# Sums of an output weight's blocks: from GpSimd in SBUF to copies and accumulating transfers from DRAM to DRAM

## The chip, the cores and the metric

One core of a Trainium2 chip. The metric is the device time of one execution in microseconds (us), taken as the median of several runs. Loads, stores and the transfers between DRAM tensors (DMA) run on 16 DMA engines that all queues of the core share. The engines are called here by the names of the profile: PE (TensorE), PEld (its weight loads), DVE (VectorE), ACT (ScalarE), POOL (GpSimd) and SP (SyncE, which issues nearly all DMAs; "SPq" in the rows).

## The reference, cut to what matters

A layer with two groups of heads over 1024 tokens and a model width of 2048, all in float32:

```python
h = einsum('bsd,de->bse', x, w_in)            # 1024 x 2048 by 2048 x 5392
q_a, k_a, v_a, z_a, q_g, k_g, v_g, z_g, gk_lr = split(h, ...)
y_a = sliding_window_attention(rope(q_a), rope(k_a), v_a, sinks) * silu(z_a)
y_g = rmsnorm(gated_linear_attention(q_g, k_g, v_g, decay(gk_lr))) * silu(z_g)
y = einsum('bse,ed->bsd', concatenate([y_a, y_g], -1), w_out)   # 1024 x 2048 by 2048 x 2048
out = layer_norm(2 ** 0.25 * x + y, ln_g, ln_b)
```

## The kernel before

**Products.** Each float32 operand of a large product is split into two parts (`split`, lines 109 to 114): ACT casts it to a high part (L112), DVE subtracts that from the operand to get the low part (L113). Each product is then three matmuls, high by high, high by low and low by high.

**Input projection.** The work is a list of jobs, one column block of `w_in` each, in the order of the string `ORDER`: K V q0 k0 v0 a0 z0 and so on, once for each half of the tokens. Jobs 0 and 1 (K and V) run together; job 2 is q0, job 3 is k0, job 4 is v0. An ordinary job is 48 matmuls of 128x512 (`main_f`, L172 to L174); a job of kind "v" is 192 matmuls of 128x256 (`main_v`, L186 to L188). The weights of a job come by SP in loads of 512 KB (`load`, L103) into the four buffers `raw`, and the split parts go to the eight buffers of `w_p`, which hold two ordinary jobs' worth. Attention and the linear attention run between the jobs' matmuls on all engines.

**Output projection.** It is one level of Strassen's scheme (Winograd's form): seven products instead of eight, over the quarters of y and of `w_out`, in the order `seq = (1, 6, 7, 4, 5, 3, 2)`. Products 4 to 7 take a combination of the weight's blocks b11, b12, b21, b22; products 1 to 3 take a block as it is. y is kept in DRAM (`yd`) and loaded again; `y_part` makes the combinations of y's blocks on POOL (L721, L717), and `collect` adds the finished sums to the residual.

**The weight's combinations** are made beforehand by `weight_sums` (L626 to L639), which is called 32 times between the jobs of the projection, after every second job from job 6 on. A call loads four pieces of 128x256 (L634, 128 KB each) into one `raw` buffer, does four subtractions on POOL (L635 to L638) and stores the four results with one DMA of 512 KB to the DRAM tensor `td` (L639). In `w_part` products 4 to 7 read them from there (L736) in runs of 1 KB.

**What sets the order.** The program is handed to a scheduler, which places each instruction in its engine's queue by the program's order, by priorities (`tc.high_priority`) and by what it takes to be ready. On the chip each queue runs in order. Semaphores order what depends on each other; SP's DMAs use eight semaphores in turn, and a DMA waits until the DMA that had its semaphore before, eight DMAs ahead, has landed.

```python
def weight_sums(n):
    f, k, u = n // 16, n % 16 // 2, n % 2
    ...
    for t, (eg, q) in ((b11, (f, 0)), (b12, (2 + f, 0)), (b21, (f, 2)), (b22, (2 + f, 2))):
        SP.dma_start(t, w_out[eg, q + k // 4][:, c])
    G.tensor_tensor(b11, b12, b11, ALU.subtract)
    ...
    SP.dma_start(td[f][:, n % 16], r)
```

Of the kernel before, what the change touches and what calls it, by code (L numbers as in the profile page):

```python
# [7 lines left out]
F32 = mybir.dt.float32  # L8
# [3 lines left out]
ALU = mybir.AluOpType  # L12
# [4 lines left out]
P = 128  # L17
S = 1024
D = 2048
T = 512  # L20
# [55 lines left out]
def build(ctx: ExitStack, tc, xT, xr, w_e, w_v, w_gk, w_up, b_gk, cos_d, sin_d, cst_d, sinks, wn_d, w_out, g_d, b_d, out):  # L76
    nc = tc.nc
    V, A, G, PE, SP = nc.vector, nc.scalar, nc.gpsimd, nc.tensor, nc.sync

    raw_p = ctx.enter_context(tc.tile_pool(name="raw", bufs=4))  # L80
    w_p = ctx.enter_context(tc.tile_pool(name="wsp", bufs=8))
    x_p = ctx.enter_context(tc.tile_pool(name="xsp", bufs=16))
    dr_p = ctx.enter_context(tc.tile_pool(name="ydram", bufs=1, space=DRAM))
# [73 lines left out]
    G.tensor_copy(al, acc_a.rearrange('p c i -> p (c i)').unsqueeze(1).to_broadcast([P, NB, P]))  # L157


    td = [dr_p.tile([P, 16, 4, 256], F32, name=f"td{f}") for f in range(2)]  # L160
    ys_d = dr_p.tile([P, 8 * T], F32, name="ysum")
    yd = [[dr_p.tile([P, 4 * T], F32, name=f"yd{H}_{q}") for q in range(4)] for H in range(2)]


    def main_f(ws, xs):
        accs = [mm.tile([P, T], F32, name="acc", tag="mm") for _ in ws]
        for k in range(KT):
            xh, xl = xs[k]
            c = slice((k % 4) * P, (k % 4) * P + P)
            for acc, w in zip(accs, ws):  # L170
                wh, wl = w[k // 4]
                PE.matmul(acc, wh[:, c], xh, start=(k == 0), stop=False)  # L172
                PE.matmul(acc, wh[:, c], xl, start=False, stop=False)  # L173
                PE.matmul(acc, wl[:, c], xh, start=False, stop=(k == KT - 1))  # L174
        return accs

    def main_v(w, xs):
        acc = [mm.tile([P, 2, 256], F32, name="accv", tag="mm") for _ in range(2)]
        for k in range(KT):
            wh, wl = w[k // 2]  # L180
            c = slice((k % 2) * 256, (k % 2) * 256 + 256)
            xh, xl = xs[k]
            for tb in range(NB):
                o = acc[tb // 2][:, tb % 2]
                t = slice(tb * P, tb * P + P)
                PE.matmul(o, xh[:, t], wh[:, c], start=(k == 0 and tb % 2 == 0), stop=False, skip_group_check=True)  # L186
                PE.matmul(o, xh[:, t], wl[:, c], start=False, stop=False, skip_group_check=True)  # L187
                PE.matmul(o, xl[:, t], wh[:, c], start=False, stop=(k == KT - 1), skip_group_check=True)  # L188
        return acc
# [117 lines left out]
    def low_rank(acc, wgk, k, r):  # L307

        u = k % 4
        PE.matmul(acc[32 * u:32 * u + 32], wgk[:, 32 * k:32 * k + 32], r, start=(k < 4), stop=(k >= 12), tile_position=(0, 32 * u), skip_group_check=True)  # L310
# [132 lines left out]
    def order(ins, head):  # L443
        with_dep = mybir.DependencyInfo(mybir.DependencyClass.NoSync, mybir.DependencyReason.DATA)
        tc.add_manual_dep(ins.ins, head.ins.name, with_dep, reason="after the bank's first")
        return ins
# [120 lines left out]
    def evac_lr(H):  # L567
        acc = ctxs[H].pop("lracc")
        lr = cp.tile([P, T], F32R, name="lr", tag="lr")
        A.copy(lr, acc)  # L570
        V.scalar_tensor_tensor(lr, lr.bitcast(F32), cst[:, C_DUP:C_DUP + 1], acc, ALU.mult, ALU.add)
        ctxs[H]["lr"] = lr
# [4 lines left out]
    n = len(jobs)  # L577
# [46 lines left out]
        load_tabs(H)  # L624
        return xr

    def weight_sums(n):

        f, k, u = n // 16, n % 16 // 2, n % 2
        c = slice((k % 4) * 512 + u * 256, (k % 4) * 512 + u * 256 + 256)  # L630
        r = raw_p.tile([P, 4, 256], F32, name="raw", tag="raw")
        b11, b12, b21, b22 = r[:, 0], r[:, 1], r[:, 2], r[:, 3]
        for t, (eg, q) in ((b11, (f, 0)), (b12, (2 + f, 0)), (b21, (f, 2)), (b22, (2 + f, 2))):
            SP.dma_start(t, w_out[eg, q + k // 4][:, c])  # L634
        G.tensor_tensor(b11, b12, b11, ALU.subtract)  # L635
        G.tensor_tensor(b12, b22, b12, ALU.subtract)
        G.tensor_tensor(b22, b22, b11, ALU.subtract)
        G.tensor_tensor(b21, b21, b22, ALU.subtract)  # L638
        SP.dma_start(td[f][:, n % 16], r)  # L639

    def get(i):
        if i not in parts:
            parts[i] = [w for src in jobs[i].src for w in load_split(src, w_p, "w")]
        return parts.pop(i)
# [6 lines left out]
        for f in due:  # L651
            f()

    i = 0
    while i < n:
        H = jobs[i].H
        if i in (0, n0):
            xr0 = begin(H, i)
        group = [i, i + 1] if i in paired else [i]
        ws = [get(j) for j in group]  # L660
        if jobs[i].kind == "v":
            accs = [main_v(ws[0], ctxs[H]["x"])]
        else:
            accs = main_f(ws, ctxs[H]["x"])
        if i == 0:
            for k in range(KT):
                low_rank(ctxs[0]["lracc"], ctxs[0]["wgk"], k, xr0[k])
        if i in (0, n0):
            evac_lr(H)
        if i == 0:  # L670
            x0.close()
            gp = side.enter_context(tc.tile_pool(name="gp", bufs=1, reuse_waits="tile"))
        run_later()
        for j, acc in zip(group, accs):
            if jobs[j].evac:
                jobs[j].evac(acc)
            for at, f in enumerate(jobs[j].later):
                if f and at == 0:
                    f()
                elif f:  # L680
                    pending.append((at - 1, f))
        if i > 5 and i % 2 == 0 and i // 2 - 3 < 32:
            weight_sums(i // 2 - 3)
        i += len(group)
    while pending:
        run_later()
# [14 lines left out]
    def y_raw(h, g, k, tag):  # L701

        r = x_p.tile([P, T], F32, name="yr", tag=tag)
        with tc.high_priority(2000):
            SP.dma_start(r, yd[h][2 * g + k // 4][:, (k % 4) * T:(k % 4 + 1) * T])
        return r

    def y_part(i, k):

        at = {1: "00", 2: "01", 3: "01", 4: "11", 5: "10", 6: "10", 7: "00"}[i]  # L710
        a = y_raw(int(at[0]), int(at[1]), k, "xh")
        kept = ys_d[:, k * T:k * T + T]
        if i == 3:
            b = x_p.tile([P, T], F32, name="yr", tag="xl")
            with tc.high_priority(2000):
                SP.dma_start(b, kept)
            G.tensor_tensor(a, a, b, ALU.subtract)  # L717
        more = {5: ((1, 1, 1),), 6: ((1, 1, 1), (0, 0, -1)), 7: ((1, 0, -1),)}
        for n, (h, g, sign) in enumerate(more.get(i, ())):
            b = y_raw(h, g, k, "xl" if n % 2 == 0 else "xh")  # L720
            G.tensor_tensor(a, a, b, ALU.add if sign > 0 else ALU.subtract)  # L721
        if i == 6:
            A.dma_start(kept, a)
        return split(a, x_p, "x")

    def w_part(i, fp, q, pool, tag):

        r = raw_p.tile([P, 2, 512], F32, name="raw", tag="raw")
        with tc.high_priority(2000):
            if i in (1, 2, 3):  # L730
                eg, w = {1: (fp, 0), 2: (fp, 2), 3: (2 + fp, 2)}[i]
                src = w_out[eg, w + q // 2][:, (q % 2) * 1024:(q % 2) * 1024 + 1024]
                SP.dma_start(r, src.rearrange("p (u c) -> p u c", u=2))
            else:
                j = {5: 0, 7: 1, 4: 2, 6: 3}[i]
                SP.dma_start(r.rearrange("p u (h c) -> p (u h) c", h=2), td[fp][:, 4 * q:4 * q + 4, j])  # L736
        return [split(r[:, u], pool, tag) for u in range(2)]

    def product(acc, y, w, t, k, first, last):
# [44 lines left out]
    def collect(i, fp, t, acc):  # L784
        lo, hi = slice(fp * 512, fp * 512 + 512), slice(1024 + fp * 512, 1024 + fp * 512 + 512)
        c11, c12, c21, c22 = pre[t][:, lo], pre[t][:, hi], pre[NB + t][:, lo], pre[NB + t][:, hi]
        if i == 1:
            V.scalar_tensor_tensor(c11, c11, ALPHA, acc, ALU.mult, ALU.add)
        elif i == 6:
            A.copy(c12, acc)  # L790
        elif i == 7:
            A.copy(c22, acc)
        elif i == 4:
            V.scalar_tensor_tensor(c21, c21, ALPHA, acc, ALU.mult, ALU.add)
            stat(NB + t, fp)
        elif i == 5:
            V.tensor_tensor(c22, c22, acc, ALU.add)
            stat(NB + t, 2 + fp)
        elif i == 3:
            V.tensor_tensor(c12, c12, acc, ALU.add)  # L800
            stat(t, 2 + fp)
        else:
            V.tensor_tensor(c11, c11, acc, ALU.add)
            stat(t, fp)
# [15 lines left out]
    for n, i in enumerate(seq[:-1]):  # L820
        if i in (1, 4):
            for t in range(NB):
                tb = t + (NB if i == 4 else 0)
# [30 lines left out]
    for ts in ((0, 1), (2,), (3,)):  # L854
        acc = {(t, fp): a for t in ts for fp, a in zip(range(2), banks(2))}
# [56 lines left out]
```

## Time and profile before

| | |
|---|---|
| time, median of 3 runs | 1437.69 us (1437.56 to 1438.25) |
| the profiled execution: time | 1435.88 us |
| its span, first to last instruction | 1433.7 us |
| PE busy | 1414.9 us, 99% |
| DVE, ACT, POOL busy | 856.7, 600.3, 290.3 us |
| moved by DMA | 222.36 MB |

The profile is of one execution, whose own time is 2.2 us more than its span and 1.8 us less than the median of the runs. In its rows a time is that of the instruction's start, from the span's start; "x2" after an instruction says that so many stand together. A matmul's shown duration reaches beyond the start of the next one, since matmuls are pipelined: the pace is read from the distance of the starts. A line number belongs to kernel.py before the change.

### The profile page before, as it was taken

How to read it: one execution, taken by the hardware profiler on the slowest of the kernel's cores; microseconds unless marked ns; L12 is line 12 of the kernel's file. 1: busy time of each engine (PE TensorE's matmuls, PEld its weight loads, DVE VectorE, ACT ScalarE, POOL GpSimd, SP SyncE). 2: the span in 40 equal slices, each digit the busy share in tenths (PEclk: the TensorE clock that was granted, in tenths of full speed). 3: DMA queues.
4: the chain of work that ended last, by engine and by line, in shares of the span. 5: the costliest groups of instructions: out<-in, count | busy, mean ns of one | idle time of the engine just before them, and what ended most of it. 6: DMA issues, size and time to landing. Idle time of an engine off the chain costs nothing.

```text
span 1433.7 us, 23435 instructions
## 1 busy us (share of the span) xinstructions
PE 1414.9 (99%) x8992; PEld 1181.0 (82%) x8992; DVE 856.7 (60%) x1481; ACT 600.3 (42%) x1279; POOL 290.3 (20%) x325
## 2 busy tenths in 40 slices
PE   8999999999999999999999999999999999999996
PEld 5888889888888976898888888988898888888885
DVE  5565556555655566565655555564566645466798
ACT  5544435435443445344435443443545324433320
POOL 0032212221311122213212221131101412122000
PEclk9999999999999999999999999999999999999998
DMA  8243344443434435543443334433325797665552
GB/s 318 86 148 128 111 147 131 135 133 107 144 131 134 133 127 175 168 157 113 159 133 123 115 131 136 138 112 118 104 95 163 239 362 230 216 218 189 172 208 117
DMA packets 99231, 222.36 MB, mean 155 GB/s; under 512 B 10800, under 2 KB 43568, under 8 KB 97968
## 3 DMA queue, kind: packets, MB, share of 16 engines
q1 hardware_dynamic: 97968, 218.78, 46.1%
q10 hardware_dynamic: 1152, 2.10, 0.4%
q8 instruction: 70, 1.15, 0.3%
q14 instruction: 41, 0.34, 0.1%
HBM read 180.47 MB, written 35.65 MB: 151 GB/s over the span
## 4 chain that ended last, share of the span: by engine, by line
PE 98%; DVE 1%; DMA 1%; ACT 0%; POOL 0%; SPq 0%; issue 0%; DVEq 0%; POOLq 0%
PE acc L172 18%; PE acc L174 18%; PE acc L173 17%; PE acco L742 7%; PE acco L743 7%; PE acco L744 7%; PE accv L186 4%; PE accv L188 4%; PE accv L187 4%; PE po L291 2%; PE pa L360 1%; PE ps L259 1%; PE ps L260 1%; PE pt L281 1%; PE lracc L310 1%; PE pg L405 1%
## 5 line engine op out<-in xcount | busy, mean ns | idle before, releaser
L113 DVE TENSOR_TENSOR wl<-raw,wh 128x512 fp32r<-128x512 f32 x440 | 331.6, 759 | 280.7 <-ACT wh L112 258.1
L112 ACT CAST wh<-raw 128x512 fp32r<-128x512 f32 x440 | 269.8, 620 | 416.9 <-PE acc L173 283.5
L172 PE MATMUL acc<-xh,wh 128*128 128x512 f32 x1088 | 429.4, 396 | 6.5 <-ACT wh L112 6.5
L174 PE MATMUL acc<-xh,wl 128*128 128x512 f32 x1088 | 427.1, 393 | 0.0
L173 PE MATMUL acc<-xl,wh 128*128 128x512 f32 x1088 | 426.9, 393 | 0.0
L172 PEld LDWEIGHTS acc<-xh,wh 128*128 128x128 f32 x1088 | 205.0, 188 | 53.8 <-ACT wh L112 8.4
L174 PEld LDWEIGHTS acc<-xh,wl 128*128 128x128 f32 x1088 | 204.8, 188 | 44.8 <-issue 1.4
L173 PEld LDWEIGHTS acc<-xl,wh 128*128 128x128 f32 x1088 | 205.0, 188 | 42.6 <-issue 2.2
L743 PE MATMUL acco<-wl,xh 128*128 128x512 f32 x416 | 161.9, 389 | 0.0
L742 PE MATMUL acco<-wh,xh 128*128 128x512 f32 x416 | 160.7, 390 | 0.2
L744 PE MATMUL acco<-wh,xl 128*128 128x512 f32 x416 | 160.8, 389 | 0.0
L186 PE MATMUL accv<-wh,xh 128*128 128x256 f32 x512 | 145.3, 284 | 0.0
L188 PE MATMUL accv<-wh,xl 128*128 128x256 f32 x512 | 145.0, 283 | 0.0
L187 PE MATMUL accv<-wl,xh 128*128 128x256 f32 x512 | 144.8, 283 | 0.0
L186 PEld LDWEIGHTS accv<-wh,xh 128*128 128x128 f32 x512 | 98.1, 192 | 1.2 <-issue 0.7
L188 PEld LDWEIGHTS accv<-wh,xl 128*128 128x128 f32 x512 | 98.1, 192 | 0.6 <-issue 0.3
L187 PEld LDWEIGHTS accv<-wl,xh 128*128 128x128 f32 x512 | 98.2, 192 | 0.5
L742 PEld LDWEIGHTS acco<-wh,xh 128*128 128x128 f32 x416 | 78.1, 188 | 17.3 <-ACT xh L112 1.3
L744 PEld LDWEIGHTS acco<-wh,xl 128*128 128x128 f32 x416 | 78.1, 188 | 16.7 <-DVE xl L113 0.4
L743 PEld LDWEIGHTS acco<-wl,xh 128*128 128x128 f32 x416 | 78.1, 188 | 15.8
L113 DVE TENSOR_TENSOR xl<-yr,xh 128x512 fp32r<-128x512 f32 x56 | 38.5, 687 | 77.4 <-ACT xh L112 76.9
L112 ACT CAST xh<-yr 128x512 fp32r<-128x512 f32 x56 | 34.6, 620 | 118.4 <-POOL yr L721 66.9
(169 smaller groups left out, 1686.7 us busy)
## 6 DMA issues: line engine op xcount, KB each, us to landing
raw<-in_w_e_dram SPq DMA_DIRECT2D x134, 512.0 KB, 3.9
yr<-yd SPq DMA_DIRECT2D x88, 256.0 KB, 4.8
raw<-in_w_v_dram SPq DMA_DIRECT2D x32, 512.0 KB, 4.2
raw<-in_w_out_dram SPq DMA_DIRECT2D x128, 128.0 KB, 2.7
td<-raw SPq DMA_DIRECT2D x32, 512.0 KB, 3.5
raw<-td SPq DMA_DIRECT2D x32, 512.0 KB, 4.6
raw<-in_w_out_dram SPq DMA_DIRECT2D x24, 512.0 KB, 4.0
raw<-in_xT_dram SPq DMA_DIRECT2D x15, 512.0 KB, 4.7
```

Source lines behind the costliest of these rows:

```text
L112: A.copy(hi, src)
L113: V.tensor_tensor(lo, src, hi.bitcast(F32), ALU.subtract)
L172: PE.matmul(acc, wh[:, c], xh, start=(k == 0), stop=False)
L173: PE.matmul(acc, wh[:, c], xl, start=False, stop=False)
L174: PE.matmul(acc, wl[:, c], xh, start=False, stop=(k == KT - 1))
L186: PE.matmul(o, xh[:, t], wh[:, c], start=(k == 0 and tb % 2 == 0), stop=False, skip_group_check=True)
L187: PE.matmul(o, xh[:, t], wl[:, c], start=False, stop=False, skip_group_check=True)
L188: PE.matmul(o, xl[:, t], wh[:, c], start=False, stop=(k == KT - 1), skip_group_check=True)
L291: x = PE.matmul(po[64 * u:64 * u + 64, a:b], vt[:, j + 1, 64 * g:64 * g + 64], pms[u][:, a2:b2], start=(len(heads) < 2), stop=(j == NB - 1 ...
L742: PE.matmul(acc, yh[:, c], wh, start=(first and k == 0), stop=False, skip_group_check=True)
L743: PE.matmul(acc, yh[:, c], wl, start=False, stop=False, skip_group_check=True)
L744: PE.matmul(acc, yl[:, c], wh, start=False, stop=(last and k == 7), skip_group_check=True)
```

## The change

The sums are made without SBUF and without POOL's arithmetic. Each of the 16 tensors `td[i, f, q]` (128x2048 float32, 1 MB, for product i in 5, 7, 6, 4, half f of the columns and half q of the rows) is begun by one plain copy of 1 MB of `w_out` from DRAM to DRAM, issued by SP (`sum_begin`, in the program after every third job from job 6 on), and ended by one accumulating transfer of 1 MB from DRAM to DRAM, issued by POOL (`sum_end`, after every third job from job 11 on). Transfers only add, so where a difference was needed, the signs move to the sums of y (`y_part`, add and subtract change places, as many operations as before) and to the copies from PSUM (`collect`, `A.mul` by -1 for `A.copy`). `w_part` reads the sums in runs of 4 KB. The call `order(...)` behind the accumulating transfer is a hint to the scheduler without a semaphore: it places the transfer behind the head of a job's matmuls.

```diff
-    td = [dr_p.tile([P, 16, 4, 256], F32, name=f"td{f}") for f in range(2)]
+    td = {(i, f, q): dr_p.tile([P, 4 * T], F32, name=f"td{i}{f}{q}") for i in (4, 5, 6, 7) for f in range(2) for q in range(2)}
...
-    def weight_sums(n):
-
-        f, k, u = n // 16, n % 16 // 2, n % 2
-        c = slice((k % 4) * 512 + u * 256, (k % 4) * 512 + u * 256 + 256)
-        r = raw_p.tile([P, 4, 256], F32, name="raw", tag="raw")
-        b11, b12, b21, b22 = r[:, 0], r[:, 1], r[:, 2], r[:, 3]
-        for t, (eg, q) in ((b11, (f, 0)), (b12, (2 + f, 0)), (b21, (f, 2)), (b22, (2 + f, 2))):
-            SP.dma_start(t, w_out[eg, q + k // 4][:, c])
-        G.tensor_tensor(b11, b12, b11, ALU.subtract)
-        G.tensor_tensor(b12, b22, b12, ALU.subtract)
-        G.tensor_tensor(b22, b22, b11, ALU.subtract)
-        G.tensor_tensor(b21, b21, b22, ALU.subtract)
-        SP.dma_start(td[f][:, n % 16], r)
+    sums = [(i, f, q) for i in (5, 7, 6, 4) for f in range(2) for q in range(2)]
+
+    def sum_begin(i, f, q):
+        eg, c = {5: (f, q), 7: (2 + f, q), 6: (2 + f, 2 + q), 4: (f, 2 + q)}[i]
+        SP.dma_start(td[i, f, q], w_out[eg, c])
+
+    def sum_end(i, f, q, behind):
+        src = {5: w_out[2 + f, q], 7: w_out[2 + f, 2 + q], 6: td[5, f, q], 4: td[6, f, q]}[i]
+        order(G.dma_start(td[i, f, q], src, accum_op=ALU.add, max_dma_last_dim=4096), behind)
...
-        if i > 5 and i % 2 == 0 and i // 2 - 3 < 32:
-            weight_sums(i // 2 - 3)
+        if i > 5 and i % 3 == 0 and started < len(sums):
+            sum_begin(*sums[started])
+            started += 1
+        if i > 8 and i % 3 == 2 and ended < started:
+            sum_end(*sums[ended], job_head[0])
+            ended += 1
...
+        first, *more = {1: ((0, 0),), 2: ((0, 1),), 3: ((0, 1),), 4: ((1, 1),), 5: ((1, 0), (1, 1)),
+                        6: ((1, 0), (1, 1), (0, 0)), 7: ((0, 0), (1, 0))}[i]
+        a = y_raw(*first, k, "xh")
         if i == 3:
...
+            G.tensor_tensor(a, a, b, ALU.add)
+        for n, (h, g) in enumerate(more):
+            b = y_raw(h, g, k, "xl" if n % 2 == 0 else "xh")
             G.tensor_tensor(a, a, b, ALU.subtract)
...
-                j = {5: 0, 7: 1, 4: 2, 6: 3}[i]
-                SP.dma_start(r.rearrange("p u (h c) -> p (u h) c", h=2), td[fp][:, 4 * q:4 * q + 4, j])
+                src = td[i, fp, q // 2]
+            SP.dma_start(r, src[:, (q % 2) * 1024:(q % 2) * 1024 + 1024].rearrange("p (u c) -> p u c", u=2))
...
         elif i == 6:
-            A.copy(c12, acc)
+            A.mul(c12, acc, -1.0)
         elif i == 7:
-            A.copy(c22, acc)
+            A.mul(c22, acc, -1.0)
```

The order of the instructions moves at two places. The first is SP's queue right behind the loads of the first jobs' weights and of the tables cos and sin. Before, the load of job 3's weights (`raw<-in_w_e_dram`) and of job 4's (`raw<-in_w_v_dram`) stand there:

```order
L560 DMA sin<-in_sin_dram 128x512
L103 DMA raw<-in_w_e_dram 128x1024 x2
L103 DMA raw<-in_w_v_dram 128x1024 x3
L206 DMA rs<-rq 32x512 x2
L103 DMA raw<-in_w_v_dram 128x1024
L206 DMA rs<-rq 32x512 x2
```

In the changed program the scheduler has brought all 16 copies forward to this place, since they wait for nothing that the program makes. Behind sin come first seven more rows like the first one here (`td_114` to `td_117` and `td_122` to `td_124`):

```order
L636 DMA td_125<-in_w_out_dram 16x16384
L103 DMA raw<-in_w_e_dram 128x1024
L636 DMA td_118<-in_w_out_dram 16x16384
L103 DMA raw<-in_w_e_dram 128x1024
L636 DMA td_119<-in_w_out_dram 16x16384
L636 DMA td_120<-in_w_out_dram 16x16384
L636 DMA td_121<-in_w_out_dram 16x16384
L636 DMA td_110<-in_w_out_dram 16x16384
L636 DMA td_111<-in_w_out_dram 16x16384
L636 DMA td_112<-in_w_out_dram 16x16384
L636 DMA td_113<-in_w_out_dram 16x16384
L103 DMA raw<-in_w_v_dram 128x1024 x2
```

So the first half of job 3's weights stands behind 8 copies, the second half behind 9, and job 4's behind all 16.

The second place is POOL's queue at the first sums. `s<-s,sm` is the scaling of the attention's probabilities, which PE transposes next. Before, the four subtractions of a call stand around it:

```order
L635 TENSOR_TENSOR raw<-raw 128x256
L278 TENSOR_TENSOR s<-s,sm 128x512
L636 TENSOR_TENSOR raw<-raw 128x256
L637 TENSOR_TENSOR raw<-raw 128x256
L638 TENSOR_TENSOR raw<-raw 128x256
L208 TENSOR_TENSOR rs<-rs,sin 128x512
```

In the changed program single accumulating transfers stand there, 16 in the whole queue:

```order
L282 TENSOR_TENSOR s<-s,sm 128x512
L640 DMA td_114<-in_w_out_dram 256x1024
L282 TENSOR_TENSOR s<-s,sm 128x512
L212 TENSOR_TENSOR rs<-rs,sin 128x512
L640 DMA td_115<-in_w_out_dram 256x1024
L282 TENSOR_TENSOR s<-s,sm 128x512 x2
```

Each takes the place of two calls' eight subtractions.

## Rows read from the trace of the kernel before

**Rows 1.** The page: span, then busy time of each engine, share and instructions.
```profile
span 1433.7 us, 23435 instructions
PE 1414.9 (99%) x8992; PEld 1181.0 (82%) x8992; DVE 856.7 (60%) x1481; ACT 600.3 (42%) x1279; POOL 290.3 (20%) x325
```
**Rows 2.** The waits of PE: line, releaser: us in total, times, longest.
```profile
PE acc L172 <- ACT wh L112: 6.5, 1, 6.5
```
**Rows 3.** The chain of waits at both ends: start us, us, what.
```profile
1.18 4.62 DMA raw<-in_w_e_dram
5.82 0.63 ACT wh L112
6.49 0.80 PE acc L172
...
1416.15 0.69 DVE pre L803
```
**Rows 4.** The timeline of SP, first loads and last stores: start, length, what.
```profile
19.94 0.33 SPq L139 DMA_DIRECT2D wn<-in_wn_dram  x1
...
22.51 0.33 SPq L560 DMA_DIRECT2D sin<-in_sin_dram  x1
23.83 1.25 SPq L103 DMA_DIRECT2D raw<-in_w_e_dram  x2
...
1381.37 5.76 SPq L768 DMA_DIRECT2D out_dram<-pre  x4
```
**Rows 5.** DMA issues: count, KB each, median us from issue to landing.
```profile
rs<-rq SPq DMA_DIRECT2D x72, 64.0 KB, 3.6
...
sin<-in_sin_dram SPq DMA_DIRECT2D x1, 256.0 KB, 4.4
...
wn<-in_wn_dram SPq DMA_DIRECT2D x1, 1.0 KB, 6.1
```
**Rows 6.** Windows: stretch, length, busy time of each engine, clock, DMA share, GB/s.
```profile
15.00:20.00 5.00, 5.00 (x25) 2.76 (x24) 3.98 (x7) 4.22 (x9) 0.00 (x0) 1.00 1.00 401
1390.00:1395.00 5.00, 5.00 (x24) 4.14 (x23) 5.00 (x9) 0.02 (x1) 0.00 (x0) 1.00 1.01 423
...
800.00:1000.00 200.00, 200.00 (x1321) 168.40 (x1322) 113.77 (x216) 86.31 (x198) 44.57 (x56) 1.00 0.39 129
1200.00:1360.00 160.00, 159.83 (x703) 131.25 (x702) 97.86 (x145) 59.64 (x108) 30.67 (x22) 1.00 0.65 207
```
**Rows 7.** The timeline of PE: its first matmuls, job 3's head, job 4's head.
```profile
11.35 0.63 PE L174 MATMUL acc<-xh,wl 128*128 128x512 f32 x1
11.77 0.73 PE L172 MATMUL acc<-xh,wh 128*128 128x512 f32 x2
...
48.79 0.39 PE L172 MATMUL acc<-xh,wh 128*128 128x512 f32 x1
49.02 0.39 PE L173 MATMUL acc<-xl,wh 128*128 128x512 f32 x1
...
60.64 0.29 PE L186 MATMUL accv<-wh,xh 128*128 128x256 f32 x1
```
**Rows 8.** The groups of POOL and ACT: line, what, count | busy us, mean ns.
```profile
L638 POOL TENSOR_TENSOR raw<-raw 128x256 f32<-128x256 f32 x32 | 29.7, 929 | 2.4
...
L635 POOL TENSOR_TENSOR raw<-raw 128x256 f32<-128x256 f32 x32 | 24.5, 765 | 241.6 <-DMA raw<-in_w_out_dram 227.9 <-DVE wl L113 4.6 <-DVE sza L303 4.6
...
L508 ACT ACTIVATE kq<-acc 128x512 f32<-128x512 f32 x8 | 4.7, 591 | 0.0
L790 ACT COPY pre<-acco 128x512 f32<-128x512 f32 x8 | 4.5, 588 | 1.8 <-PE acco L744 1.6
```
**Rows 9.** The timeline of POOL and of PE at one sum: the scaling, then its transposes.
```profile
123.09 1.04 POOL L278 TENSOR_TENSOR s<-s,sm 128x512 f32<-128x512 f32 x1
...
126.69 0.60 PE L281 MATMUL pt<-cst,s 128*128 128x128 f32 x4
```
**Rows 10.** The waits of SP: line, releaser: us in total, times, longest.
```profile
SPq L103 <- DVE wl L113: 287.0, 83, 9.2
```

More of the change, by code (lines that the diff above doesn't have):

```diff
@@ L157, in build @@
     G.tensor_copy(al, acc_a.rearrange('p c i -> p (c i)').unsqueeze(1).to_broadcast([P, NB, P]))
-    td = [dr_p.tile([P, 16, 4, 256], F32, name=f"td{f}") for f in range(2)]
+    td = {(i, f, q): dr_p.tile([P, 4 * T], F32, name=f"td{i}{f}{q}") for i in (4, 5, 6, 7) for f in range(2) for q in range(2)}
     ys_d = dr_p.tile([P, 8 * T], F32, name="ysum")
     yd = [[dr_p.tile([P, 4 * T], F32, name=f"yd{H}_{q}") for q in range(4)] for H in range(2)]
+    job_head = [None]
     def main_f(ws, xs):
@@ L171, in main_f @@
                 wh, wl = w[k // 4]
-                PE.matmul(acc, wh[:, c], xh, start=(k == 0), stop=False)
+                first = PE.matmul(acc, wh[:, c], xh, start=(k == 0), stop=False)
+                job_head[0] = first if k == 0 else job_head[0]
                 PE.matmul(acc, wh[:, c], xl, start=False, stop=False)
@@ L185, in main_v @@
                 t = slice(tb * P, tb * P + P)
-                PE.matmul(o, xh[:, t], wh[:, c], start=(k == 0 and tb % 2 == 0), stop=False, skip_group_check=True)
+                first = PE.matmul(o, xh[:, t], wh[:, c], start=(k == 0 and tb % 2 == 0), stop=False, skip_group_check=True)
+                job_head[0] = first if k == 0 else job_head[0]
                 PE.matmul(o, xh[:, t], wl[:, c], start=False, stop=False, skip_group_check=True)
@@ L652, in run_later @@
             f()
-    i = 0
+    i, started, ended = 0, 0, 0
     while i < n:
@@ L708, in y_part @@
     def y_part(i, k):
-        at = {1: "00", 2: "01", 3: "01", 4: "11", 5: "10", 6: "10", 7: "00"}[i]
-        a = y_raw(int(at[0]), int(at[1]), k, "xh")
         kept = ys_d[:, k * T:k * T + T]
+        first, *more = {1: ((0, 0),), 2: ((0, 1),), 3: ((0, 1),), 4: ((1, 1),), 5: ((1, 0), (1, 1)),
+                        6: ((1, 0), (1, 1), (0, 0)), 7: ((0, 0), (1, 0))}[i]
+        a = y_raw(*first, k, "xh")
         if i == 3:
@@ L716, in y_part @@
                 SP.dma_start(b, kept)
+            G.tensor_tensor(a, a, b, ALU.add)
+        for n, (h, g) in enumerate(more):
+            b = y_raw(h, g, k, "xl" if n % 2 == 0 else "xh")
             G.tensor_tensor(a, a, b, ALU.subtract)
[L718 to L721, printed above, removed]
         if i == 6:
@@ L731, in w_part @@
                 eg, w = {1: (fp, 0), 2: (fp, 2), 3: (2 + fp, 2)}[i]
-                src = w_out[eg, w + q // 2][:, (q % 2) * 1024:(q % 2) * 1024 + 1024]
-                SP.dma_start(r, src.rearrange("p (u c) -> p u c", u=2))
-            else:
-                j = {5: 0, 7: 1, 4: 2, 6: 3}[i]
-                SP.dma_start(r.rearrange("p u (h c) -> p (u h) c", h=2), td[fp][:, 4 * q:4 * q + 4, j])
+                src = w_out[eg, w + q // 2]
+            else:
+                src = td[i, fp, q // 2]
+            SP.dma_start(r, src[:, (q % 2) * 1024:(q % 2) * 1024 + 1024].rearrange("p (u c) -> p u c", u=2))
         return [split(r[:, u], pool, tag) for u in range(2)]
```

## The prediction

> **What bounds the kernel now.** I read the page first. PE is busy 1414.9 of 1433.7 us, 99%, and POOL, which the change relieves most, 20% [rows 1]. In the list of waits PE then has one wait of more than a moment: 6.5 us at the start, for the first cast of a weight [rows 2]. The chain of waits shows that this is the way of the first load: it lands at 5.8, ACT casts, PE starts at 6.49; at the other end DVE takes over from PE at 1416.15 and finishes the last row of the output [rows 3]. So the idle time of PE, 18.8 us, lies before the first matmul and behind the last one, and the change touches neither. In the output projection, where the changed loads of `td` are used, PE is busy 159.83 of 160 us [rows 6]. What can be gained there is 0.2 us; what PE loses anywhere is lost for good. The question is only whether PE has to wait for something now.
>
> The place to look at is where the new copies stand: behind sin, ahead of the weights of jobs 3 and 4. Before, sin is issued at 22.51 and lands 4.4 us later, at 26.9, and job 3's loads follow at 23.83 [rows 4, 5]. PE begins job 3 at 48.79 and job 4 at 60.64 [rows 7], so those weights had 20 us and more to spare.
>
> That a load behind the copies really waits for them is seen on the constants: `wn`, 1 KB, takes 6.1 us to land, while a rope transfer of 64 KB takes 3.6 as a rule [rows 5]. The small one was queued behind loads of 512 KB at a time when the DMA engines were fully busy, and did not overtake them. SP also issues those constants 1.3 us apart where an issue takes 0.33 [rows 4]: each waits for the landing of the DMA eight before it.
>
> **The 16 copies.** Each moves 1.049 MB. The trace has no transfer from DRAM to DRAM, so I bound it by its two legs. Loads from DRAM with all DMA engines busy move 401 GB/s (15 to 20 us); the stores of the result to DRAM, four of 1 MB, move 423 GB/s (1390 to 1395 us) [rows 4, 6]. A leg is 1.049 MB / 401 = 2.6 us for the read and 1.049 / 423 = 2.5 us for the write. If the legs overlap wholly, a copy costs 2.6 us; if DRAM does no more in both directions together than it is seen to do in one, 5.1 us. I take 5.1: a copy has both legs in DRAM, which no load and no store has, and no window shows DRAM moving more than 423 GB/s in total.
>
> A load of 512 KB at 401 GB/s takes 1.3 us, and from a landing to the first matmul it is 6.49 - 5.80 = 0.7 us [rows 3]. Then, counted from sin's landing at 26.9:
>
> - Job 3 has its first weights behind 8 copies and one load: 26.9 + 8 x 5.1 + 1.3 + 0.7 = 69.7 instead of 48.8. PE stands still for 21 us. The second half lands behind 9 copies and two loads, at 75.4 us, and is usable at 76.1; with 24 matmuls at 0.23 us behind it, job 3 ends at about 82.
> - Job 4 has its weights behind all 16 copies and three loads: 26.9 + 16 x 5.1 + 3 x 1.3 + 0.7 = 113.1 instead of 60.6. PE waits again, 31 us.
>
> The two waits do not add to more than the second arrival: the whole delay at job 4 is 113.1 - 60.6 = **52.5 us**. From there the loads come without copies between them, and as nothing on PE has slack, the delay stays until the end.
>
> The Trainium skill has a rate for such copies: "DMA: Bandwidth & Descriptors", section "Latency and other measured facts", gives 207 to 214 GB/s per direction for copies between two tensors in HBM with plain queues. An estimate by the upper figure: 4.9 us a copy, a delay of 49 us, 1489 us in all; no run here shows it yet. The same page, section "Bandwidth", puts one core's limit at the HBM at about 358 GB/s; an estimate by it, both legs one after the other and the loads at that rate too: 5.9 us a copy, a delay of 65 us, 1505 us. This case's trace does not agree with that limit: it has 401 and 423 GB/s in single windows, so the sum stays with those.
>
> **Restart.** At the start of the kernel the first 12 matmuls of PE begin 0.44 us apart ((11.77 - 6.49) / 12) and the following ones 0.23 us apart [rows 3, 7]: after its idle time PE ran at half pace for 5.3 us, although the granted clock of those windows reads 1.00. After 31 us of idle time I expect the same once more, 5.3 - 12 x 0.23 = **2.5 us**. The same restart of job 3 costs nothing, since job 4 waits for its weights anyway.
>
> **The 16 accumulating transfers on POOL.** A POOL DMA is not in the trace. For issuing one I take between the 0.33 us of an SP issue [rows 4] and the 3.4 us of the four subtractions of one call (from 0.77 to 0.93 us each [rows 8]). Each transfer replaces two calls, 6.8 us of POOL, so POOL's queue holds less in both cases: 0 on the path. What waits behind it on POOL is the scaling of the probabilities, and behind that PE's transposes; at one such place the scaling ends at 124.13 and the transposes begin at 126.69, 2.6 us later [rows 9]. That is the cover, and a POOL issue of more than 2.6 us just ahead of a scaling would be seen on PE (a rival below). The data: two reads and one write, 3 legs, some 7.6 us of the DMA engines each, 122 us in all over about 900 us of a projection in which the engines are busy 39% [rows 6]; what goes away is 32 calls of 1 MB of loads and stores, 32 x 2.6 = 83 us. Loads are mostly early: SP spent 287 us waiting until DVE freed a buffer for the next weights [rows 10]. With two jobs' worth of split weights held, a transfer of 7.6 us hides behind 11 us of matmuls per job. I cost them at 0.
>
> **Edits with one answer.** The sums of y have as many POOL operations as before, add for subtract: 0. `A.mul` for `A.copy`, 16 times: 591 against 588 ns in like shape [rows 8], off the path: 0. Loads of `td` in runs of 4 KB: at best the 0.2 us above.
>
> **Sum.** 1435.9 us (the profiled execution's own time) + 52.5 + 2.5 = 1490.9; the median of the runs is 1.8 us above that execution, so 1492.7, and I say **1492 us**.
>
> **Rivals.**
>
> 1. *The copies' legs overlap.* For it: each DMA engine reads and writes at once in any load. Against it: DRAM would have to move some 800 GB/s. At 2.6 us a copy job 3 is late by 1 us only, job 4 starts at 26.9 + 41.6 + 3.9 + 0.7 = 73.1, 12.5 us late; with the restart 15 us, **1453 us**.
> 2. *Not slower: the copies are out of the way in time.* A copy does not go through SBUF, so it might be faster than either leg as seen. The point that decides is (60.6 - 26.9 - 3.9 - 0.7) / 16 = 1.8 us a copy; below it job 4's weights are there when PE wants them, and the time stays at **1438 us**. Against it: 1.8 us is 580 GB/s in each direction, above every window of the trace.
> 3. *POOL's issue is long.* If POOL is held 3.4 us by each transfer, the scaling behind it is 0.8 us later than PE's slack allows, 16 times: 13 us more, **1505 us**. For it: in the changed order a scaling follows nearly every transfer. Against it: subtractions just as long stood there 32 times without a wait of PE.
>
> **How the numbers follow.** The forecast gets 0.67, rival 1 0.15, rival 2 0.06, rival 3 0.12. The forecast's own range takes 20% on the price of a copy for what the trace cannot show (reads beside writes, runs of 64 KB): 4.1 to 6.1 us give a delay of 36.5 to 68.5 us, 1477 to 1509. The whole range reaches down to rival 1, 1452, and up past rival 3 taken alone, to 1512; rival 2 and the far ends are left out. A difference of 0.2%, 2.9 us, is about what a measurement of this kernel tells from none. Slower by more than that: all but rival 2, 0.94. Within it 0.05, faster 0.01, since no idle time of PE is within the change's reach.
>
> **What would show it.** Right: in the waits of PE two new long ones at the heads of jobs 3 and 4, released by an ACT cast that waited for its load, some 21 and 31 us; in the windows from 27 to 110 us DMA engines fully busy and PE mostly idle; the landings of the copies 5 us apart; after job 4's head every job as late as the one before it, and a tail as long as now. Wrong: landings 2.6 us apart or less; job 4's load landing before copies issued ahead of it; waits of PE at the transposes spread over the whole projection, released by POOL (rival 3); or PE waiting for weights long after 120 us, which would mean that the accumulating transfers are not hidden.

## The result and the profile after

The changed kernel takes **1462.0 us** (4 runs, 1460.67 to 1463.0) against 1437.62 us of the kernel before beside it: a ratio of 1.0172, 95% interval 1.0155 to 1.019. It is slower, as forecast, but by 24 us and not by 54; the time lies inside the range of 1452 to 1512, a sixth of the way up, and the forecast's own range (1477 to 1509) missed it.

The page of the changed kernel, with the lines that answer to [rows 1] and the queue of POOL's DMAs (packets, MB, share of the DMA engines' time):

```profile
span 1460.8 us, 23047 instructions
...
PE 1418.9 (97%) x8992; PEld 1184.9 (81%) x8992; DVE 841.2 (58%) x1481; ACT 598.8 (41%) x1279; POOL 196.6 (13%) x213
...
q0 software_dynamic: 4352, 16.78, 6.4%
```

The span grew by 27.1 us; that is a little more than the 24 us between the medians, since the profiled execution of the kernel before was 1.8 us faster than its median. PE's busy time accounts for 4.0 of it (1418.9 for 1414.9), the rest is idle time of PE. Where, is told by the waits of PE, to be held against the single line of [rows 2]:

```profile
PE accv L189 <- ACT wh L112: 15.6, 1, 15.6
PE acc L174 <- ACT wh L112: 13.3, 2, 6.7
PE acco L746 <- ACT xh L112: 0.8, 1, 0.8
```

The two waits on L174 are the one at the start (6.6) and a new one of 6.7 us; with 15.6 and 0.8 the new ones make 23.1 us, and 23.1 + 4.0 is the 27.1. The timeline of ACT shows what the casts themselves waited for:

```profile
54.77 1.14 ACT L112 CAST wh<-raw 128x512 fp32r<-128x512 f32 x2 [5.43 <-DMA raw<-in_w_e_dram]
...
83.26 1.14 ACT L112 CAST wh<-raw 128x512 fp32r<-128x512 f32 x2 [14.30 <-DMA raw<-in_w_v_dram]
```

And the timeline of PE, where the last matmul of job 2, the head of job 3 and the head of job 4 answer to [rows 7] (48.79 and 60.64 before):

```profile
48.32 0.39 PE L177 MATMUL acc<-xh,wl 128*128 128x512 f32 x1
55.44 0.79 PE L174 MATMUL acc<-xh,wh 128*128 128x512 f32 x1 [6.74 <-ACT wh L112]
...
83.93 0.80 PE L189 MATMUL accv<-wh,xh 128*128 128x256 f32 x2 [15.59 <-ACT wh L112]
```

So the loss is where it was forecast, at the heads of jobs 3 and 4, released by a cast that waited for its load. Job 4 begins 83.93 - 60.64 = 23.3 us later.

The price of a copy is read from landings, one issue at a time. The rows are the first copy, the last copy, the first load of job 3 and the first of job 4, each with its start and its time to landing:

```profile
L636 SPq DMA_DIRECT2D td<-in_w_out_dram x1: 616/616/616, 23.4 to 23.4; - x1
DMA to landing us min/median/max: 6.7/6.7/6.7
...
L636 SPq DMA_DIRECT2D td<-in_w_out_dram x1: 489/489/489, 57.2 to 57.2; - x1
DMA to landing us min/median/max: 22.7/22.7/22.7
...
L103 SPq DMA_DIRECT2D raw<-in_w_e_dram x1: 337/337/337, 30.1 to 30.1; - x1
DMA to landing us min/median/max: 24.6/24.6/24.6
...
L103 SPq DMA_DIRECT2D raw<-in_w_v_dram x1: 334/334/334, 58.5 to 58.5; - x1
DMA to landing us min/median/max: 24.6/24.6/24.6
```

The first copy lands at 30.1, the last at 79.9. Between them lie 15 copies and job 3's two loads of 1.3 us: (49.8 - 2.6) / 15 = **3.1 us a copy**, where the forecast had 5.1. That is 1.049 MB / 3.1 us, about 335 GB/s read and 335 GB/s written at the same time. Job 4's load lands at 83.1, 3 us behind the last copy.

### The profile page after: what moved, and what is told of

It is laid out like the page before. It is cut to its first block, busy times and chain, and to the rows that moved or that the text cites. A ratio compares the mean times of both kernels' runs of the same rounds, so it can differ in the third digit from the quotient of the medians.

```text
span 1460.8 us, 23047 instructions
## 1 busy us (share of the span) xinstructions
PE 1418.9 (97%) x8992; PEld 1184.9 (81%) x8992; DVE 841.2 (58%) x1481; ACT 598.8 (41%) x1279; POOL 196.6 (13%) x213
## 3 DMA queue, kind: packets, MB, share of 16 engines
q0 software_dynamic: 4352, 16.78, 6.4%
## 4 chain that ended last, share of the span: by engine, by line
PE 90%; DMA 7%; DVE 1%; POOL 0%; issue 0%; ACT 0%; SPq 0%; DVEq 0%; POOLq 0%; ACTq 0%
PE acc L174 16%; PE acc L177 16%; PE acc L176 16%; PE acco L748 6%; PE acco L747 6%; PE acco L746 6%; PE accv L189 4%; PE accv L192 4%; PE accv L191 4%; PE po L295 2%; DMA raw<-in_w_e_dram 2%; DMA raw<-in_w_v_dram 2%; PE pa L364 1%; DMA yr<-yd 1%; PE ps L263 1%; PE ps L264 1%
## 5 line engine op out<-in xcount | busy, mean ns | idle before, releaser
L113 DVE TENSOR_TENSOR wl<-raw,wh 128x512 fp32r<-128x512 f32 x440 | 322.8, 741 | 312.7 <-ACT wh L112 299.1
L174 PE MATMUL acc<-xh,wh 128*128 128x512 f32 x1088 | 430.2, 396 | 13.3 <-ACT wh L112 13.3
L174 PEld LDWEIGHTS acc<-xh,wh 128*128 128x128 f32 x1088 | 205.2, 189 | 61.4 <-ACT wh L112 14.7
L189 PE MATMUL accv<-wh,xh 128*128 128x256 f32 x512 | 146.2, 286 | 15.6 <-ACT wh L112 15.6
L189 PEld LDWEIGHTS accv<-wh,xh 128*128 128x128 f32 x512 | 99.3, 194 | 16.8 <-ACT wh L112 16.0
## 6 DMA issues: line engine op xcount, KB each, us to landing
td<-in_w_out_dram POOLq DMA_DIRECT2D x8, 1024.0 KB, 10.5
```

The source lines that it names most:

```text
L113: V.tensor_tensor(lo, src, hi.bitcast(F32), ALU.subtract)
L174: first = PE.matmul(acc, wh[:, c], xh, start=(k == 0), stop=False)
L189: first = PE.matmul(o, xh[:, t], wh[:, c], start=(k == 0 and tb % 2 == 0), stop=False, skip_group_check=True)
```

## The experiments

Each was timed beside the kernel before; a ratio is to its time there. Theory Q is the prediction's with the price corrected: the loss is the arrival of the weights of jobs 3 and 4 behind copies in one queue, 3.1 us each, and nothing else.

**e1: copies spread out.** The hint that `sum_end` has is given to the copies too:

```diff
-    def sum_begin(i, f, q):
+    def sum_begin(i, f, q, behind):
...
-        SP.dma_start(td[i, f, q], w_out[eg, c])
+        order(SP.dma_start(td[i, f, q], w_out[eg, c]), behind)
...
-            sum_begin(*sums[started])
+            sum_begin(*sums[started], job_head[0])
```

> The changed kernel, but each copy is placed in SP's queue behind the head of the job after which the program has it, one copy at a time over the whole projection, so no load of weights stands behind more than one copy. Theory Q (the loss is the arrival of the weights of jobs 3 and 4 behind 8 to 16 copies in one queue, and nothing else costs): 1438 us, within 3 us of the kernel before, one long wait of PE only, the 6.5 us at the start. Rival R (part of the loss is the extra DRAM traffic, the accumulating transfers or POOL's issue, wherever the copies stand): 1445 us or more, with PE waits spread over the projection.

Measured: 1435.38 us, ratio to before 0.9987 (0.9978 to 0.9997). The waits of PE in this kernel, then its copies, all 16, with their least, median and longest time to landing:

```profile
PE acc L174 <- ACT wh L112: 6.4, 1, 6.4
PE pa L364 <- issue: 0.5, 1, 0.5
```

```profile
L636 SPq DMA_DIRECT2D td<-in_w_out_dram x16: 512/518/542, 93.2 to 792.3; - x16
DMA to landing us min/median/max: 6.1/7.3/8.6
```

The same 16 copies and 16 accumulating transfers, issued from 93 to 792 us, cost nothing. All of the loss is in the place of the copies; rival R has fallen. The kernel is at least as fast as the one before: the interval of 0.03 to 0.22% below it excludes 1 only just, and the spans of the two profiled executions (1433.8 and 1433.7) do not show where a gain would lie. It is the version to keep of the changed kind.

**e2: eight copies at the front.** As e1, but only for half of the sums:

```diff
-        SP.dma_start(td[i, f, q], w_out[eg, c])
+        copy = SP.dma_start(td[i, f, q], w_out[eg, c])
+        if i in (6, 4):
+            order(copy, behind)
```

> The 8 copies for products 5 and 7 stay in front of job 3's weights, the other 8 are placed behind job heads as in e1. Theory Q with the copies' landings of the changed kernel (the eighth at 52.3 us): job 3's first weights land at 54.7 instead of job 4's at 83.2, job 3 starts at about 55.4 instead of 48.8, 6.7 us late, 2 to 2.5 us for the restart at half pace, and job 4's weights are there in time: 1447 us (1445 to 1449). Rival R: no nearer to before than the share of copies moved would make it, 1450 to 1462 us.

Measured: 1446.17 us, ratio 1.0069 (1.0044 to 1.0094). The waits of PE:

```profile
PE acc L174 <- ACT wh L112: 12.7, 2, 6.7
PE acco L748 <- ACT xh L112: 3.5, 2, 3.1
```

The new wait on L174 is 12.7 - 6.7 = 6.0 us at the head of job 3, where the cast starts at 54.1, and job 4 has none. The arithmetic of arrivals holds: 9 us for the eight copies in front of job 3, and the other 15 us of the change belong to the eight in front of job 4. The 3.5 us in the output projection are not explained; the profiled execution is the slowest of the four, 4 us above the median, so they may be that execution's alone.

**e3: no accumulating transfers.** `sum_end` returns before it issues anything, so the second addend of every sum is left out.

> The changed kernel without its 16 accumulating transfers; the copies stay at the front. This leaves out the second addend of every sum of weight blocks. Theory Q: the transfers are hidden, 1462 us within 2 us. Rival R (they cost by POOL's issue or by taking DMA time from the loads): 1455 us or less; at the extreme of the prediction's rival 3, 0.8 us each, 13 us less.

Measured: 1461.76 us, ratio 1.0172 (1.0149 to 1.0195), as with them. POOL's side of them is read in the changed kernel itself: POOL is held 0.86 to 1.07 us by the issue of one, and it lands after 9.5 us as a median:

```profile
L640 POOL DMA_DIRECT2D td<-in_w_out_dram x8: 887/945/1073, 183.5 to 476.6; - x8
L640 POOL DMA_DIRECT2D td<-td x8: 857/923/954, 511.1 to 846.1; - x8
...
DMA to landing us min/median/max: 7.8/9.5/12.3
```

**e4: copies in runs of 4 KB.**

```diff
-        SP.dma_start(td[i, f, q], w_out[eg, c])
+        SP.dma_start(td[i, f, q], w_out[eg, c], max_dma_last_dim=4096)
```

> The changed kernel with each copy in 256 runs of 4 KB instead of 16 runs of 64 KB. What sets the price of a copy, 3.1 us in the changed kernel? Theory L (the read and the write overlap and together meet a limit of DRAM or of the DMA engines, whatever the length of the runs): landings 3.1 us apart as before, 1462 us within 3 us. Rival (the long runs make the copy cheap, the 5.1 us of the prediction would hold for runs as short as the loads'): landings 4 to 5 us apart and 1476 to 1492 us.

Measured: 1464.16 us, ratio 1.0191 (1.0171 to 1.0211); against the changed kernel the intervals overlap. The first copy is issued at 23.7 and lands after 7.1 us, at 30.8; the last two are these:

```profile
L636 SPq DMA_DIRECT2D td<-in_w_out_dram x2: 3072/3516/3960, 55.3 to 59.3; - x2
DMA to landing us min/median/max: 21.9/22.9/23.8
```

The one issued at 59.3 takes 21.9 us and lands at 81.2. That is (50.4 - 2.6) / 15 = 3.2 us a copy. The length of the runs is not what makes the copy cheaper than I had priced it.

**e5: copies on POOL's queue.** This was to show that the loads were late because of the queue they shared. A small POOL copy that reads sin's table holds the first issue back until sin has landed:

```diff
+    marker = cp.tile([P, 1], F32, name="marker")
+    mark = []
...
-        SP.dma_start(td[i, f, q], w_out[eg, c])
+        if not mark:
+            mark.append(G.tensor_copy(marker, ctxs[0]["tabs"][1][:, :1]))
+        order(G.dma_start(td[i, f, q], w_out[eg, c]), mark[0])
```

> The 16 copies at the same time as in the changed kernel (their first issue waits for sin's landing), but issued by POOL, on its own queue; SP's queue holds only the loads. Theory Q (the loads were late because they stood behind the copies in one queue): the loads of jobs 3 and 4 land about as in the kernel before, later loads share the DMA engines with the copies until about 80 us and still come in time; 1438 us (1436 to 1442), no long wait of PE after the start. Rival B (50 us of busy DMA engines delay every load, in whichever queue the copies stand): PE waits at job 3, 4 or 5, 1447 us or more.

Measured: 1464.55 us, ratio 1.0195 (1.0177 to 1.0213): a clear miss of theory Q as I had put it. Nothing stands ahead of the loads in SP's queue now, and the time is that of the changed kernel. The waits of PE have one new long line. Why, is told by the rows of job 4's second and third load together, of SP's queue between the third and the fourth, and of the fourth (before, the fourth was issued at 38.4 and landed after 4.2 us):

```profile
PE vtp L235 <- ACT va L230: 20.5, 1, 20.5
```

```profile
L103 SPq DMA_DIRECT2D raw<-in_w_v_dram x2: 327/354/382, 25.9 to 32.9; - x2
DMA to landing us min/median/max: 18.3/23.5/28.8
...
37.46 1.22 SPq L210 DMA_DIRECT2D rs<-rq  x2
...
L103 SPq DMA_DIRECT2D raw<-in_w_v_dram x1: 522/522/522, 38.8 to 38.8; - x1
DMA to landing us min/median/max: 47.0/47.0/47.0
```

The second load lands 18.3 us after its issue, at 44.2, the third at 61.7 and the fourth at 85.8. In ACT's queue the casts of that fourth load stand ahead of the copy of `va`, for which PE waits; in ACT's timeline they start at 85.82, casts that need the rope transfers (`rs<-rq`) issued beside it follow from 90.27, and `va` at 94.04. A load has 128 rows of 4 KB, eight on each of 16 DMA engines; a copy has one run of 64 KB on each (this kernel's page counts 4864 packets on q0, 512 more than the changed kernel's 4352, that is 16 copies x 16 engines x one run and one completion). I read the 24 us between the last two landings as eight copies' time: if an engine takes turns between two queues run by run, eight small runs cost eight turns of one copy each. That became theory T, and the next two kernels tested it. The two rope transfers that stand between these loads I had overlooked.

**e8 and e9: POOL's queue with shorter runs.** As e5, with

```diff
-        order(G.dma_start(td[i, f, q], w_out[eg, c]), mark[0])
+        order(G.dma_start(td[i, f, q], w_out[eg, c], max_dma_last_dim=4096), mark[0])
```

and 32768 in place of 4096 in e9.

> As e5, the copies on POOL's queue at the same time, but each in 256 runs of 4 KB instead of 16 runs of 64 KB. In e5 a load of 512 KB took 24 to 29 us while the copies ran, about as long as 8 copies. Theory T (each DMA engine takes turns between the two queues run by run: a load has 8 runs of 4 KB on each engine, so beside runs of 64 KB it needs 8 turns of one copy each, beside runs of 4 KB only 8 equal turns): the loads land in 3 to 8 us, no PE wait behind the start, 1438 us (1436 to 1443). Rival B (the busy DMA engines delay the loads whatever the runs): the fourth load of job 4 lands after the copies again, 1455 to 1465 us.

> As e5, with runs of 32 KB. Theory T: a load needs 8 turns of half a copy each, 12 to 15 us instead of 24 to 29; two loads per job then take a little longer than a job of matmuls, and the delay shrinks to between 0 and 10 us, 1438 to 1448 us. Rival B: as e5, 1460 us or more.

Measured: e8 1441.62 us, ratio 1.0037 (1.0023 to 1.005); e9 1451.12 us, ratio 1.01 (1.0079 to 1.0121), 3 us above its expected range. The fourth load of job 4 in e8, then the second and third together and the fourth in e9, and behind them PE's longest new wait in e9:

```profile
L103 SPq DMA_DIRECT2D raw<-in_w_v_dram x1: 600/600/600, 39.0 to 39.0; - x1
DMA to landing us min/median/max: 8.8/8.8/8.8
```

```profile
L103 SPq DMA_DIRECT2D raw<-in_w_v_dram x2: 328/350/372, 26.1 to 32.4; - x2
DMA to landing us min/median/max: 14.1/16.3/18.5
...
L103 SPq DMA_DIRECT2D raw<-in_w_v_dram x1: 521/521/521, 38.3 to 38.3; - x1
DMA to landing us min/median/max: 29.4/29.4/29.4
```

```profile
PE vtp L235 <- ACT va L230: 7.9, 1, 7.9
```

The same bytes at the same time on the same queue, and only the length of a run differs: 8.8, 29.4 and 47.0 us to landing for runs of 4, 32 and 64 KB, and 5, 14 and 28 us more than before. So rival B has fallen: how long a load waits beside copies on another queue goes by the length of their runs. The count in theory T was not right, though. These are the packets of POOL's queue (q0) and of SP's (q1), first in e5 from 44 to 62 us, then in e9 from 40 to 66, in which loads and copies are waiting all the time:

```profile
q0 software_dynamic: 174, 5.64, 90.2%
q1 hardware_dynamic: 175, 0.45, 8.9%
...
q0 software_dynamic: 369, 8.00, 83.9%
q1 hardware_dynamic: 367, 1.05, 16.1%
```

The engines took as many packets from one queue as from the other, while q0 moved 12 times the bytes in e5 and 8 times in e9. A packet is one run or one completion. On each engine a load is then nine packets, eight runs and a completion, while a copy is two in e5 and three in e9 (5120 packets on q0, 768 more than 4352). So one load passes in the time of 4.5 copies in e5 and of 3 in e9. The copies land from 35.2 to 86.5 us in e5 and from 35.9 to 88.1 in e9, 3.4 and 3.5 us apart, which gives 15 and 10.5 us. From the second load's landing to the third's it is 17.5 us in e5 and 10.7 in e9 (40.2 to 50.9). The fourth load has the two rope transfers ahead of it, each 32 rows and so two runs and a completion on each engine: 15 packets in all, 7.5 copies or 26 us in e5, 5 copies or 17 us in e9, and 24.1 and 16.8 us were measured. That eight copies' time came so near in e5 was luck.

Two things stay open. Beside runs of 4 KB a load took 8.8 to 9.7 us, more than the 3 to 8 expected and more than equal turns with such short runs explain. And e8 has no long wait, but several of 0.5 to 1.7 us, most of them at the linear attention's operands; where its 5 us come from was not followed further.

**e6: the burst later.** As e1, but all 16 copies on SP's queue behind the head of one later job.

```diff
-        if i > 5 and i % 3 == 0 and started < len(sums):
-            sum_begin(*sums[started])
-            started += 1
+        if i == 9:
+            for x in sums:
+                sum_begin(*x, job_head[0])
+            started = len(sums)
```

> All 16 copies again in one burst on SP's queue, but later, behind the head of the program's tenth job, where the loads run ahead of PE by all the buffers they have (4 raw ones and two jobs' split weights, about four jobs). Theory Q with cover: the burst of 16 x 3.1 = 50 us meets some 40 to 50 us of weights in hand instead of the 29 us between the burst's start and job 4; 0 to 10 us of delay, 1437 to 1448 us. Rival (a burst costs the same anywhere): 24 us, 1460 us.

Measured: 1452.23 us, ratio 1.0109 (1.0094 to 1.0124), between the two expectations. One new wait of PE, 11.6 us, makes most of it. First PE's waits on L174, then the load that stands in the middle of the burst and the one behind it:

```profile
PE acc L174 <- ACT wh L112: 18.3, 2, 11.6
```

```profile
L103 SPq DMA_DIRECT2D raw<-in_w_e_dram x1: 333/333/333, 141.6 to 141.6; - x1
DMA to landing us min/median/max: 27.0/27.0/27.0
...
L103 SPq DMA_DIRECT2D raw<-in_w_e_dram x1: 334/334/334, 172.2 to 172.2; - x1
DMA to landing us min/median/max: 30.6/30.6/30.6
```

A burst costs less here than at the front. The loads were further ahead: the burst begins at 134.3 and PE's wait at 191.9, 58 us later, where in the changed kernel it is 25 us (23.4 to 48.7). But it is not hidden: the second load is not even issued before 172.2, because SP stands at the copies, each of which waits for the landing of the DMA eight before it, and then it needs 30.6 us more, to 202.8.

**e7: the write leg alone.** Stores of 1 MB from SBUF in place of the copies:

```diff
-        SP.dma_start(td[i, f, q], w_out[eg, c])
+        SP.dma_start(td[i, f, q].rearrange("p (u c) -> p u c", u=4), wuph.bitcast(F32).unsqueeze(1).to_broadcast([P, 4, T]))
```

> Each copy replaced by a store of 1 MB from SBUF to the same DRAM tensor, so the write leg alone in a burst of ten and more. This leaves out the first addend of every sum of weight blocks (a constant tile is stored in its place), and the scheduler places the stores behind job 4's first loads, so the time says little; the landings are what is read. If the write leg sets a copy's 3.1 us, the stores land 3.1 us apart; if a copy is a fifth dearer than either leg because both legs meet in DRAM, they land 2.5 us apart, as the 423 GB/s of the result's stores says. Time about 1438 us, since job 4's weights stand ahead of the burst.

Measured: the first store is issued at 26.4 and lands after 9.6 us, at 36.0; the ninth, issued at 43.7, lands 12.8 us later, at 56.5: (56.5 - 36.0) / 8 = 2.6 us a store. The tenth lands 3.4 us behind the ninth, at 59.9. The rows are the first one and the ninth and tenth together:

```profile
L636 SPq DMA_DIRECT2D td<-wuph x1: 632/632/632, 26.4 to 26.4; - x1
DMA to landing us min/median/max: 9.6/9.6/9.6
...
L636 SPq DMA_DIRECT2D td<-wuph x2: 2480/2496/2512, 43.7 to 46.3; - x2
DMA to landing us min/median/max: 12.8/13.2/13.6
```

The write leg alone is about what [rows 6] gave, 2.5, and a copy with both legs is a fifth dearer, not twice as dear. The time, 1448.45 us, missed the expected 1438: PE waited 8.3 us for operands of the linear attention; the cause of that was not followed further, since this kernel's place of the stores is another.

## Why the prediction was right or wrong

- **The bound, the place and the mechanism** were right. PE had no idle time to give, the two waits came at the heads of jobs 3 and 4, released by casts that waited for loads, and nothing was made up later. e1 and e2 show that the place of the copies is the whole of the loss. The waits were 6.7 and 15.6 us and not 21 and 31, in the main by the price of a copy.
- **The price of a copy is the step that failed**: "if DRAM does no more in both directions together than it is seen to do in one, 5.1 us. I take 5.1". It measured 3.1. No window that I read of the trace before had reads and writes at full rate together, and I took the highest sum I had seen for a limit. The legs overlap for the most part: 2.6 us for a read leg by [rows 6], 2.6 for the write leg in e7, 3.1 for both. With 3.1 the prediction's own line gives 26.9 + 16 x 3.1 + 3 x 1.3 + 0.7 = 81.1 for job 4's head, 20.5 us late, and with the restart 1461 us; 83.93 was measured, 2.8 us more: the last copy lands 0.8 us later than in that line, and job 4's load 3.2 us behind it, not 1.3.
- **The estimate from the Trainium skill** ("DMA: Bandwidth & Descriptors", section "Latency and other measured facts", 207 to 214 GB/s per direction between tensors in HBM, there for rows of 16 KiB that lie far apart) stood close beside my 5.1 and made it look safe. The measurement decides: about 335 GB/s per direction here, at runs of 64 KB and, in e4, of 4 KB. The limit of about 358 GB/s, which the prediction took from the same page's section "Bandwidth", is there the share of a core while both cores of a pair stream; this case runs on one core, and its 401 and 423 GB/s are no contradiction to it.
- **Rival 1** (legs overlap, 1453 us) had the better mechanism and was 9 us too low. The truth lay between the two ends that I had named, nearer to the end that I gave 0.15.
- **The restart**, 2.5 us, was right. From 83.93 to 89.7 us the matmuls of job 4 start 0.21 us apart and behind that 0.12, so that 5.8 x (1 - 0.12 / 0.21) = 2.5 us were lost. In the windows of the changed kernel (columns as in [rows 6], the granted clock third from the end) it reads 0.51 from 80 to 90 us, that is 1.2 of 2.4 GHz, after PE had done nothing from 70 to 80, and 1.00 again from 90 on:

```profile
70.00:80.00 10.00, 0.00 (x0) 0.00 (x0) 0.00 (x0) 0.00 (x0) 0.00 (x0) 0.64 0.86 260
80.00:90.00 10.00, 6.07 (x27) 5.85 (x28) 5.67 (x8) 4.16 (x8) 1.46 (x1) 0.51 0.80 254
90.00:100.00 10.00, 10.00 (x84) 9.91 (x83) 7.76 (x16) 8.73 (x15) 0.00 (x0) 1.00 0.59 200
```

- **The accumulating transfers** at 0: right (e3). POOL's issue, bounded at 0.33 to 3.4 us, is 0.9; a transfer lands 9.5 us after its issue, with other traffic beside it, where I had estimated 7.6 of the DMA engines' time for its three legs. Rival 3 fell: no wait of PE in the changed kernel is released by POOL.
- **"A load behind the copies really waits for them"**: right for one queue (the changed kernel, e2, e4). But that the queue is what matters was too narrow a reading, as e5 showed; I had not asked what another queue would have done.

What stays open is what holds a copy at 3.1 us and not 2.6: DRAM with both directions busy, or the DMA engines themselves. A copy on half of the engines would tell, and was not tried.

## What to carry to other kernels

A DMA that depends on nothing moves to the front of its queue when a scheduler is let loose, and there it meets the loads for which the first jobs wait; give it a place, as one hint did here for some 26 us. Price a transfer by each leg, and take the sum of the legs only if a row shows that they do not overlap. Background transfers cost nothing here when they were spread (e1). As a burst on another queue they cost 5 us in runs as short as those of the loads beside them (e8), and 28 us in long runs (e5).

## What the runs showed of the hardware that I had not expected

- A copy from DRAM to DRAM moved about 335 GB/s in each direction, 670 GB/s in both, where loads alone moved 401 and stores alone 423.
- Two queues shared the DMA engines packet by packet, not byte by byte: 174 and 175 packets in e5, 369 and 367 in e9, a packet being one run, of 4 KB or of 64 KB alike, or one completion. The same load took 47.0, 29.4 and 8.8 us beside copies in runs of 64, 32 and 4 KB, and 4.2 us without them. The Trainium skill ("DMA: Bandwidth & Descriptors", section "Queues, rings and completion order") says that an engine takes turns between queue rows at the granularity of packets; e5 and e9 agree, with one long run as one packet.
